# First layer's memory attention: all 512 queries of a head pair in one value run, staged in the base inversion's buffer

## Chip, core and metric

The kernel runs on one core of one Trainium2 chip. Times are device microseconds (us) of one execution. The core has five engines, each with an instruction stream of its own that is worked off in order: TensorE (PE, with its weight loads shown as PEld), VectorE (DVE), ScalarE (ACT), GpSimd (POOL) and SyncE (SP), which here issues most DMAs. An instruction waits on semaphores that other engines or landed DMAs raise; while it waits, all that stands behind it on its engine waits too.

## What is computed

Two layers over 512 positions of width 1024. The first layer mixes the positions with six heads of a gated delta rule (chunks of a triangular system that must be inverted, then a scan over the chunks), the second with sliding-window attention. Each layer also lets every position attend, with four heads of width 64, to 256 memory tokens:

```python
def memory_attention(q, mem_k, mem_v):
    s = jnp.einsum("bshd,bmhd->bhsm", q, mem_k).astype(jnp.float32) * (MEM_DH ** -0.5)
    p = jax.nn.softmax(s, axis=-1).astype(q.dtype)
    o = jnp.einsum("bhsm,bmhd->bshd", p, mem_v)
    return o.reshape(q.shape[0], q.shape[1], MEM_W)
```

Behind the mixers stand an output projection, a gated feed-forward block, and at the end an RMS norm.

## The kernel before

A large product is done in three reduced-precision (fp32r) matmuls of 512 columns each (`mm3`, called from `project` and `normed`): an ACT copy makes the high part of a weight (`whi`), a DVE subtraction the low part (`wlo`), both in `split`. The projections of the first layer are accumulated in three PSUM banks `pj`. Small products (attention, delta rule) are plain fp32 matmuls, which the profile lists as two entries each; transposes are listed as one. They go to the banks `g` (two) and `sc` (three). All instructions are issued in the order of the Python calls and then rearranged by the framework's scheduler into one fixed order per engine; `nosync` adds order without a wait.

The stage around the change is in `gdn`:

- `base_inverse` (lines 690 to 727) inverts the 32x32 diagonal blocks of all 24 chunk systems at once. Its tile `big` (96 of 128 partitions used, 2048 floats wide) holds the blocks in its first half and the inverse X in its second. 31 steps of two DVE operations each (`btmp<-big`, `big<-big,btmp`) run one behind the other, mixed with other DVE work; then ACT copies X transposed into the first half (`big<-big`), and two DMAs on SP, `basex` and `basext` (line 713), store both halves to memory, from where the solve fetches them (`X64`, `Tt`, lines 720 and 725).
- `scores` makes the memory scores of a pair of heads: eight matmuls `mk,qm` into two `g` and two `sc` banks, row maxima on DVE (line 819), exponentials on ACT (L134).
- `weigh` calls `softmax` (the reciprocal) and `weighed`. In `weighed`, for each of four blocks of 128 queries: `scale` divides the weights (two tiles on DVE, line 868, or on ACT), four PE transposes (L150) turn them into a `g` bank, and one ACT copy evicts the bank into `pf`. Before the change, every two blocks four value matmuls `sc<-pf,mv` of 256 columns follow. `split` then makes the pair's result `mq` (high part on ACT, low part on DVE); it is read much later, by the output projection.
- `memory(m, ...)` runs this for the pair m = 0 and m = 1; `query` (lines 608 to 621) makes the intra-chunk products of a head (`g<-qv,kn`, then `DT<-g,DT` on DVE), `conv_tile` the convolution (one ACT copy, three DVE taps, L156), followed by a Silu on ACT.
- `solve` follows (32x32 and 64x64 products `sc<-X,N`, `sc<-Tt,Y`, with DVE evictions between them), then `values` and the scan.

The second layer (`own` true, since its banks are named `pt`) already takes all four blocks in one run of 512 columns, from a tile `pfm`.

## Time and profile before

| quantity | value |
|---|---|
| time, median of 3 runs | 1159.31 us (1158.9 to 1159.67) |
| span of the profiled execution, first to last instruction | 1155.8 us |
| what the median has over that span | 3.5 us |
| PE busy | 1142.6 us (99%) |
| DVE, ACT, POOL busy | 834.0, 626.7, 86.0 us |

The profiled execution's own total is not listed beside its span; the three timed runs lie 3.1 to 3.9 us above the span. In the rows of the timeline, the first number is the start in us from the span's start, the second the length, then engine, source line, operation, out<-in by the program's names, shapes and count; in brackets the idle time of the engine before it and who ended it. A PE entry is long because it includes the pipeline; what a matmul costs is the distance to the next entry's start.

### The profile page before, as it was taken

The numbers are of one execution on the slowest core, as the hardware profiler recorded it, in microseconds if no ns is written. First come the engines' busy times: TensorE is split into PE (matmuls) and PEld (weight loads), VectorE is DVE, ScalarE is ACT, GpSimd is POOL, SyncE is SP. The second block draws the span as 40 slices with busy tenths as digits, with TensorE's granted clock in tenths as the row PEclk, the third lists the DMA queues.
The fourth block names the chain that finished last, engine by engine and source line by source line (L and its number), as shares of the span: only waits on it lengthen the run. The fifth ranks groups of instructions, "written<-read, shape, count | busy, mean of one in ns | idle before, by whom it ended". The sixth has DMA issues, their size and how long they took to land.

```text
span 1155.8 us, 19296 instructions
## 1 busy us (share of the span) xinstructions
PE 1142.6 (99%) x7342; PEld 997.1 (86%) x7342; DVE 834.0 (72%) x1559; ACT 626.7 (54%) x1249; POOL 86.0 (7%) x97
## 2 busy tenths in 40 slices
PE   9999999999999999999999999999999999999996
PEld 7788777877899998899998877788899988999886
DVE  5664886767889877488965777839989644889554
ACT  6489672366566642266653554856666412666433
POOL 0230000000101101011100000001111000111000
PEclk9999999999999999999999999999999999999998
DMA  8244341225657636367623421117577533676232
GB/s 314 84 150 116 131 119 66 95 88 164 188 128 182 169 103 168 114 168 187 154 82 99 124 72 42 51 56 200 131 181 184 151 96 107 170 185 153 78 98 85
DMA packets 72559, 151.20 MB, mean 131 GB/s; under 512 B 16732, under 2 KB 18932, under 8 KB 72468
## 3 DMA queue, kind: packets, MB, share of 16 engines
q1 hardware_dynamic: 61060, 129.28, 35.9%
q0 software_dynamic: 11136, 20.45, 11.2%
q8 instruction: 57, 0.93, 0.3%
q14 instruction: 34, 0.28, 0.1%
q10 hardware_dynamic: 272, 0.26, 0.1%
HBM read 143.00 MB, written 6.96 MB: 130 GB/s over the span
## 4 chain that ended last, share of the span: by engine, by line
PE 93%; DVE 3%; ACT 2%; DMA 1%; issue 0%; SPq 0%; DVEq 0%; ACTq 0%
PE pj L146 43%; PE g L146 38%; PE sc L146 6%; PE qk L146 3%; PE pt L146 2%; PE pt L150 1%; PE g L150 1%; DMA wraw<-in_wmk 1%; ACT sm L134 1%; DVE qv L156 1%; DVE big L153 0%; DVE wlo L153 0%; ACT T L140 0%; DVE btmp L153 0%; DMA wraw<-in_wdn 0%
## 5 line engine op out<-in xcount | busy, mean ns | idle before, releaser
L140 ACT ACTIVATE whi<-wraw 128x512 fp32r<-128x512 f32 (+3 forms) x324 | 240.9, 750 | 254.5 <-PE pj L146 159.2
L153 DVE TENSOR_TENSOR wlo<-wraw,whi 128x512 fp32r<-128x512 f32 (+3 forms) x324 | 270.4, 844 | 100.7 <-ACT whi L140 95.2
L146 PE MATMUL pj<-h,whi 128*128 128x512 f32 (+1 forms) x652 | 257.4, 396 | 0.0
L146 PE MATMUL pj<-l,whi 128*128 128x512 f32 (+1 forms) x652 | 255.0, 392 | 0.0
L146 PE MATMUL pj<-h,wlo 128*128 128x512 f32 (+1 forms) x652 | 254.1, 391 | 0.0
L146 PE MATMUL g<-T,whi 128*128 128x256 f32 x1216 | 220.6, 282 | 0.8 <-ACT fs L140 0.8
L146 PEld LDWEIGHTS g<-T,whi 128*128 128x128 f32 x1216 | 186.9, 189 | 2.1 <-DVE fu L156 1.1
L146 PE MATMUL g<-T,wlo 128*128 128x256 f32 x608 | 171.1, 281 | 0.0
L146 PEld LDWEIGHTS pj<-h,whi 128*128 128x128 f32 x652 | 122.4, 188 | 28.6 <-issue 3.6
L146 PE MATMUL g<-h,whi 128*128 128x256 f32 (+1 forms) x500 | 146.5, 293 | 0.0
L146 PE MATMUL g<-h,wlo 128*128 128x256 f32 (+1 forms) x500 | 145.8, 292 | 0.0
L146 PE MATMUL g<-l,whi 128*128 128x256 f32 (+1 forms) x500 | 145.5, 291 | 0.0
L146 PEld LDWEIGHTS pj<-h,wlo 128*128 128x128 f32 x652 | 122.5, 188 | 25.3 <-issue 0.6
L146 PEld LDWEIGHTS pj<-l,whi 128*128 128x128 f32 x652 | 122.6, 188 | 25.2 <-issue 1.1
L146 PEld LDWEIGHTS g<-T,wlo 128*128 128x128 f32 x608 | 114.4, 188 | 0.0
L146 PEld LDWEIGHTS g<-h,whi 128*128 128x128 f32 x500 | 95.0, 190 | 2.3 <-issue 0.5
L146 PEld LDWEIGHTS g<-l,whi 128*128 128x128 f32 x500 | 94.9, 190 | 2.3 <-issue 0.5
L146 PEld LDWEIGHTS g<-h,wlo 128*128 128x128 f32 x500 | 95.0, 190 | 1.7
L1125 POOL DMA_DIRECT2D ws<-in_wgu x38 | 33.3, 875 | 712.5 <-ACT h L140 447.7
L140 ACT ACTIVATE whi<-ws 128x512 fp32r<-128x512 f32 x76 | 48.0, 631 | 49.1 <-PE g L146 41.4
L153 DVE TENSOR_TENSOR fu<-pj,rstd 128x512 f32<-128x512 f32 (+1 forms) x34 | 22.4, 660 | 53.7 <-PE pj L146 53.7
L153 DVE TENSOR_TENSOR wlo<-ws,whi 128x512 fp32r<-128x512 f32 x76 | 52.2, 687 | 7.4 <-ACT whi L140 7.2
(381 smaller groups left out, 1701.1 us busy)
## 6 DMA issues: line engine op xcount, KB each, us to landing
wraw<-in_wgu SPq DMA_DIRECT2D x50, 512.0 KB, 4.2
ws<-in_wgu SPq DMA_DIRECT2D x76, 256.0 KB, 3.6
ws<-in_wgu POOLq DMA_DIRECT2D x76, 256.0 KB, 4.7
wraw<-in_win SPq DMA_DIRECT2D x26, 512.0 KB, 3.6
wraw<-in_wdn SPq DMA_DIRECT2D x32, 384.0 KB, 3.1
wraw<-in_wdn SPq DMA_DIRECT2D x32, 320.0 KB, 3.0
wraw<-in_wgu SPq DMA_DIRECT2D x38, 256.0 KB, 4.3
wraw<-in_wout SPq DMA_DIRECT2D x16, 512.0 KB, 3.6
```

Of the source, the lines that this page charges most:

```text
L134: ins = self.nc.scalar.activation(out, in_, func, **kw).ins
L140: self.copied = self.nc.scalar.activation(out, in_, AF.Copy, **kw).ins
L146: return self.nc.tensor.matmul(out, lhsT, rhs, start=start, stop=stop, skip_group_check=more).ins
L150: return self.nc.tensor.transpose(out, in_, self.ident[:k, :k]).ins
L153: return eng.tensor_tensor(out=out, in0=a, in1=b, op=op).ins
L156: return self.nc.vector.scalar_tensor_tensor(out=out, in0=in0, scalar=scalar, in1=in1, op0=op0, op1=op1).ins
L1125: nc.gpsimd.dma_start(s1, a22, accum_op=ALU.add)
```

## The change

In the first layer a pair's four blocks are now one group: four value matmuls of 512 columns behind all sixteen transposes, instead of two times four of 256 columns behind eight transposes each. The transposed weights are no longer put into a tile `pf` of 1024 floats a partition (two such in turn for a pair, one buffer), but into a tile of 2048 floats that takes the tag, and so the one buffer, of the base inversion's `big`. The framework adds the waits that this needs: the first eviction into the buffer waits until both stores, `basex` and `basext`, have read it. The second layer's path keeps its tile and group.

```diff
-        group = NC if own else 2
+        group = NC
         for n in range(NC):
             if n % group == 0:
-                pf = {} if win else self.t(pool, [P, 2, 2, group * P], F32, "pfm" if own else "pf", 1)
+                pf = {} if win else self.t(pool, [P, 4 * T], F32, "pfm" if own else "big", 1).rearrange(
+                    "p (j b t) -> p j b t", j=2, b=2)
```

In the instruction order of the built programs, PE has eight matmuls fewer, no engine has any instruction more, and the orders differ between the first pair's transposes and the scan of the first three heads; around those, PE, DVE, ACT and SP are in the same order as before.

## Prediction

> **What bounds the kernel now.** I read the page first: the span, the busy shares, the granted clock and the chain that ended last.

> ```profile
> span 1155.8 us, 19296 instructions
> PE 1142.6 (99%) x7342; PEld 997.1 (86%) x7342; DVE 834.0 (72%) x1559; ACT 626.7 (54%) x1249; POOL 86.0 (7%) x97
> ...
> PEclk9999999999999999999999999999999999999998
> ...
> PE 93%; DVE 3%; ACT 2%; DMA 1%; issue 0%; SPq 0%; DVEq 0%; ACTq 0%
> ```

> PE is the bound: every microsecond that it works less or stands less is gained, every new stop is lost. So two questions count: how much PE work goes, and where PE stops in the new order. Next, the stage by windows (columns: window, length, busy time with entries in brackets of PE, PEld, DVE, ACT, POOL, then clock, DMA share, GB/s).

> ```profile
> 137.00:152.50 15.50, 15.44 (x83) 11.54 (x82) 15.05 (x34) 7.23 (x11) 0.00 (x0) 1.00 0.34 110
> 152.50:165.00 12.50, 11.90 (x67) 9.60 (x66) 10.29 (x27) 11.28 (x26) 0.00 (x0) 1.00 0.68 156
> ```

> The first pair's values run in the first window, while DVE is full (15.05 of 15.50) with the base inversion. The second window holds the inversion's end, the stores and the second pair's scores; there PE shows gaps. The second pair's values follow behind it.

> **Value matmuls.** PE timeline, a run of 256 columns and the entry behind it, and the second layer's run of 512 columns:

> ```profile
> 142.02 1.08 PE L146 MATMUL sc<-pf,mv 128*64 128x256 f32 x8
> 143.04 0.50 PE L146 MATMUL pj<-l,whi 128*128 128x512 f32 x1
> ...
> 712.57 1.94 PE L146 MATMUL pt<-pfm,mv 128*64 128x512 f32 x8
> 714.43 1.79 PE L146 MATMUL qk<-ks,q 64*128 64x128 f32 x16
> ```

> Start to next start, a 256 run costs 1.02, two of them 2.04; the 512 run costs 1.86. That is 0.18 less for a pair, **-0.36** for both. [...] PE goes between fp32r and fp32 matmuls 221 times in both built orders, so I count no change there; three excursions go from this stage and come back in the solve. At 0.2 to 0.3 each this leaves 0.6 either way.

> **The new wait.** The first pair's third and fourth transposes need the `g` banks that hold the first and second; these are evicted into `big`; and that eviction waits for both stores. When does PE arrive, and when does the wait end?

> ```profile
> 137.90 0.48 PE L146 MATMUL pj<-h,whi 128*128 128x512 f32 x1
> ...
> 143.84 0.40 PE L146 MATMUL pj<-l,whi 128*128 128x512 f32 x1
> ...
> 152.24 0.39 PE L146 MATMUL pj<-h,wlo 128*128 128x512 f32 x1
> ```

> The eight transposes are done at 137.90 in both orders. Behind them the new order has 105 projection matmuls (four projections of 24, nine of a fifth). From 143.84 to 152.24 37 of them went: 0.227 each. PE arrives at 137.9 + 23.8, about **161.8**.

> ```profile
> 144.54 0.68 DVE L153 TENSOR_TENSOR mq0l<-sc,mq0h 128x512 fp32r<-128x512 f32 x1
> 145.14 0.36 DVE L153 TENSOR_TENSOR btmp<-big 96x207 f32<-96x207 f32 x1
> ...
> 148.86 1.21 DVE L153 TENSOR_TENSOR wlo<-wraw,whi 128x1024 fp32r<-128x1024 f32 x1
> 149.99 0.29 DVE L153 TENSOR_TENSOR big<-big,btmp 96x135 f32<-96x135 f32 x1
> 150.20 0.74 DVE L156 SCALAR_TENSOR_TENSOR qv<-pj,gains,qv 128x511 f32<-128x511 f32 x1
> 150.86 0.26 DVE L153 TENSOR_TENSOR btmp<-big 96x112 f32<-96x112 f32 x1
> ...
> 155.57 0.18 DVE L153 TENSOR_TENSOR big<-big,btmp 96x31 f32<-96x31 f32 x1
> ```

> The inversion ended at 155.75. A 512-wide DVE operation takes 0.60 of the queue, a weight's low part 1.13, a tap 0.66. Ahead of the inversion's last step the new order loses `mq0l` and one product (-1.20) and gains two taps, one product and one low part (+3.05): 157.6 at most. Some of it falls into the short gaps between dependent steps, so I take 157.5.

> ```profile
> 140.68 1.11 ACT L140 ACTIVATE pf<-g 128x512 f32<-128x512 f32 x2 [1.00 <-PE sc L146]
> ...
> 154.77 0.62 ACT L619 ACTIVATE sq<-qv 128x512 f32<-128x512 f32 x1
> 155.78 1.99 ACT L140 ACTIVATE big<-big 96x1024 f32<-96x1024 f32 x1 [0.39 <-DVE big L153]
> 158.35 0.63 ACT L134 ACTIVATE qv<-qv 128x512 f32<-128x512 f32 x1 [0.58 <-DVE nm L160]
> 159.00 1.28 ACT L125 ACT_TABLE_LOAD   x1
> ...
> 160.76 0.47 ACT L134 ACTIVATE sm<-g,nm 128x256 f32<-128x256 f32 x1
> ```

> The stores, from the list of DMA issues (size, median us from issue to landing), with the fastest and the commonest DMA of this stage beside them:

> ```profile
> wraw<-in_win SPq DMA_DIRECT2D x26, 512.0 KB, 3.6
> ...
> q<-sq SPq DMA_DIRECT2D x6, 256.0 KB, 2.0
> ...
> basext<-big SPq DMA_DIRECT2D x1, 384.0 KB, 3.1
> ```

> On ACT, a Silu (0.63), a table load (1.28) and a square (0.62) now stand ahead of the transposing copy; the last tap that the Silu needs has one 512-wide product and seven small inversion steps (0.2 to 0.3 each) behind it on DVE, so it lies some 2.3 us ahead of the inversion's end, and the three are through at about 157.7. The copy takes 1.99, to 159.7; the `basext` store needs 3.1 more: **162.8**. An eviction takes 0.6 (two in 1.11, the second overlapping), and PE goes on at about 163.4: a stop of 1.65 us. Further on, the third eviction holds up a query product and, in the second pair, the last eviction the value run, 0.2 each: **+2.05**. The unknown is the store: it may land as early as a 256 KB store (2.0) or as late as a median weight load (3.6), which moves the stop from 0.55 to 2.15.

> Cover of the wait elsewhere: ACT waits in front of the eviction with the later evictions, the pair's high part and the second pair's exponentials behind it. No DVE work but the second pair's depends on these. The stores' SP queue has two weight loads ahead of them, for buffers freed before the inversion ends, and the `X64` fetches behind, which the solve needs some 20 us later: nothing.

> **Waits that go, and waits that come back.** PE around the second pair's scores, and the same scores of the first pair, which nothing hindered:

> ```profile
> 124.12 1.14 PE L146 MATMUL g<-mk,qm 64*128 64x256 f32 x8
> ...
> 126.05 0.50 PE L146 MATMUL pj<-h,whi 128*128 128x512 f32 x1
> ...
> 152.47 2.09 PE L146 MATMUL g<-qv,kn 128*128 128x128 f32 x16
> 154.85 0.91 PE L146 MATMUL g<-mk,qm 64*128 64x256 f32 x3 [0.30 <-DVE DT L153]
> ...
> 157.89 0.50 PE L146 MATMUL pj<-h,whi 128*128 128x512 f32 x1
> ...
> 163.47 1.05 PE L146 MATMUL g<-qv,kn 128*128 128x128 f32 x8
> 164.82 0.30 PE L150 MATMUL g<-consts,sm 128*128 128x128 f32 x1 [0.30 <-DVE sm L868]
> ```

> And the query products as a group (busy us, mean ns of one entry):

> ```profile
> L146 PE MATMUL g<-qv,kn 128*128 128x128 f32 x48 | 6.1, 277 | 0.0
> ```

> Unhindered, the scores take 1.93. Here they take 3.04 (154.85 to 157.89), so 1.1 is waiting. The sixteen entries of the query products at 152.47 start 0.12 apart (2.09 less the last one's 0.28, over 15), so the next could have started at 154.4, not 154.85: 0.45 lost, of which the row shows 0.30 as idle. By the same count 0.45 is lost ahead of 164.82. Together **-2.0** of stops in the old order that the new one does not have in these places. But it has its own: the second `g` bank of the scores waits for the second product on DVE, now behind one more 512-wide operation (0.60, plus the ACT copy that it needs), about 0.7 in all; and the third query product stands right behind the scores instead of behind 24 projection matmuls, so PE waits for one maximum (0.60), a small scaling (0.1) and two exponentials (0.47 each), less five scores (0.24 each): about 0.5 to 0.6. **+1.3**.

> **Behind the solve** the new order differs too:

> ```profile
> 208.61 0.91 PE L146 MATMUL pj<-h,wlo 128*128 128x512 f32 x2
> 209.36 0.39 PE L146 MATMUL pj<-h,whi 128*128 128x512 f32 x1
> ```

> DVE beside it, the evictions of the last solve step:

> ```profile
> 205.92 1.26 DVE L160 TENSOR_SCALAR Tt<-sc 64x256 f32<-64x256 f32 x3
> ```

> Before, nine projection matmuls stood beside DVE's three evictions (1.26), one tap (0.66) and a low part (1.13), 3.05 in all, and 0.3 was lost (0.75 for two entries of 0.227). In the new order seven projection matmuls and four transposes follow the solve's twelve matmuls, about as much PE work, while DVE has the three evictions, three taps (2.0) and the low part: 4.4, which is 1.3 more. I take 1.2 lost instead of 0.3, **+0.9**, between 0.4 (the taps fall into DVE's own waits) and 1.4 (none does).

> **Sum:** -0.36 + 2.05 - 2.0 + 1.3 + 0.9 = **+1.9 us** on the span of 1155.8, so 1157.7. The median of the runs lies 3.5 above this span (1159.31), so I predict **1161.2**.

> **Rivals.**
> *Waits do not bind* (faster): the stores land before PE arrives, the score chain's old stops (2.0) go and no new ones come, the solve stays covered. Then -0.36 - 2.0 gives 1156.9. For the store to land by 161.2 and be evicted by 161.8, ACT's copy must begin by 156.1, so the inversion must end 1.4 us earlier than I work out, and the Silu, the table load and the square must not stand ahead of it. DVE's fill, 15.05 of 15.50, speaks against it; that the old order had the inversion's end at 155.75 speaks for it. If the store alone comes in time and the rest is as computed, the sum is +0.25: 1159.6.
> *The wait is long*: the stores meet the loads of a window whose DMA share is 0.68 already and land 1.5 to 2 later, or each of the three re-placed chains costs half as much again: +3.5 to +5, about 1163.5.
> *PE slows down after the stop*: if a stop made the clock fall, matmuls of 0.227 would take longer; at half speed the fourteen projection matmuls that stand behind the scores cost 3.2 more, 1164.4. The clock's row shows nothing like it and the stage's windows have 1.00. [...]

> **How the numbers follow.** The computed case has 0.62; the store in time with the rest as computed 0.16; the long wait 0.14; the slower clock 0.02; no binding waits 0.06. The forecast's terms move it by about 1.5 either way (store 1.1 down and 0.5 up, excursions 0.6, the solve's 0.5). With the case below it and half of the long wait, the range is 1159.0 to 1163.6. A difference of 0.2% (2.3 us) is about what a measurement of this kernel can tell from no change: slower means above 1161.6, which is a third of the computed case, the long wait and the clock, 0.38; faster means below 1157.0, 0.04; within it 0.58.

> **What would show it.** In the changed profile: value runs of 512 columns at about 1.86; the inversion's last step at about 157.5; ACT's eviction into `big` ended by the `basext` DMA at about 162.8, and PE idle ahead of an L150 transpose, released by ACT, for 1 to 2 us; a gap ahead of the query product behind the second scores; a gap behind the solve at about 205 to 211. It is wrong if the stores land before 161 or PE's gap exceeds 2.5, and if PE's windows from 137 to 215 together move by less than 0.8 or more than 3.2.

## The result and the profile after

| quantity | before | after |
|---|---|---|
| time, median of 14 executions each | 1158.89 us (1157.97 to 1160.07) | 1161.99 us (1160.77 to 1169.93) |
| ratio, 95% interval | | 1.0045 (1.0035 to 1.0054) |
| span of the profiled execution | 1155.8 us | 1159.6 us |

The change costs time, clear of noise. The medians are 3.1 us apart, which is 0.27%; the ratio takes in all executions and lies nearer to that of the means (1163.85 and 1158.93). The forecast was 1161.2, with "within 0.2%" as the likeliest sign: the median lies in the range, but it is slower than that sign allowed. Two things stand beside the median. Every execution of the new kernel takes its span plus 1.7 to 1.9 us (1161.4 for the profiled one), while the prediction carried over 3.5 us from before. In the later executions of the kernel before, whose spans are on record, it is 1.7 to 2.9; so part of the 3.5 was that the profiled execution of before was a short one. And the executions of the new kernel scatter over 9 us, those of before over 2.

The page of the kernel after: PE is busy about as long as before (1143.4 us for 1142.6), but the span is 3.8 longer.

```profile
span 1159.6 us, 19269 instructions
PE 1143.4 (99%) x7326; PEld 996.4 (86%) x7326; DVE 835.1 (72%) x1559; ACT 626.4 (54%) x1249; POOL 85.1 (7%) x97
```

The same two windows as in the prediction (columns: window, length, busy time with entries of PE, PEld, DVE, ACT, POOL, then clock, DMA share, GB/s):

```profile
137.00:152.50 15.50, 15.50 (x74) 12.98 (x73) 15.18 (x32) 7.18 (x10) 0.00 (x0) 1.00 0.38 117
152.50:165.00 12.50, 10.33 (x51) 8.31 (x49) 9.26 (x20) 8.97 (x11) 0.00 (x0) 1.00 0.65 176
```

The first window has no gap left, the second lost 1.6 us of PE work (11.90 before). The timeline of PE shows where:

```profile
161.47 0.39 PE L146 MATMUL pj<-h,wlo 128*128 128x512 f32 x1
164.03 1.15 PE L150 MATMUL g<-consts,sm 128*128 128x128 f32 x8 [2.17 <-ACT big L140]
...
166.24 1.94 PE L146 MATMUL sc<-big,mv 128*64 128x512 f32 x8
168.10 1.38 PE L146 MATMUL g<-qv,kn 128*128 128x128 f32 x10
169.42 1.13 PE L146 MATMUL g<-mk,qm 64*128 64x256 f32 x4
...
172.65 1.16 PE L146 MATMUL g<-qv,kn 128*128 128x128 f32 x8
```

The stop sits where it was expected, ahead of the third transposes and released by ACT's eviction into `big`; start to start it is 2.56, which less one matmul (0.227) leaves 2.33. The run of 512 columns costs 1.86 (168.10 less 166.24). The second pair's scores take 3.23 (172.65 less 169.42), against 3.04 before and 1.93 where nothing hinders them. What DVE and ACT did before the stop:

```profile
157.07 0.19 DVE L153 TENSOR_TENSOR big<-big,btmp 96x31 f32<-96x31 f32 x1
```

```profile
157.56 2.11 ACT L140 ACTIVATE big<-big 96x1024 f32<-96x1024 f32 x1
...
162.03 0.67 ACT L140 ACTIVATE qv<-pj,gains 128x512 f32<-128x512 f32 x1
163.38 1.09 ACT L140 ACTIVATE big<-g 128x512 f32<-128x512 f32 x2 [0.67 <-ACT qv L140]
```

```profile
basext<-big SPq DMA_DIRECT2D x1, 384.0 KB, 3.6
```

The inversion ended at 157.3, the copy at 159.7; the store, issued then, took 3.6 and landed at about 163.3; the eviction began at 163.38. (The row names ACT's own operation as the releaser, but that had been done for 0.67 us: the store is what came last.)

Behind the solve, PE and DVE:

```profile
210.35 0.40 PE L146 MATMUL pj<-l,whi 128*128 128x512 f32 x1
211.03 0.47 PE L146 MATMUL pj<-h,whi 128*128 128x512 f32 x1 [0.28 <-ACT qv L140]
...
211.66 0.66 PE L150 MATMUL g<-consts,qv 128*128 128x128 f32 x4
212.98 0.50 PE L146 MATMUL pj<-h,wlo 128*128 128x512 f32 x1 [0.66 <-DVE wlo L153]
```

```profile
208.49 0.42 DVE L160 TENSOR_SCALAR Tt<-sc 64x256 f32<-64x256 f32 x1 [0.61 <-PE sc L146]
...
211.71 1.21 DVE L153 TENSOR_TENSOR wlo<-wraw,whi 128x1024 fp32r<-128x1024 f32 x1
```

From DVE's first eviction (208.49) to the end of the low part's slot (212.84, where the next operation starts) are 4.35 us; PE loses 0.45 and 0.92 there.

What the stage costs in all is read from an operation that both kernels have ahead of it and one behind it, on DVE: before first, then after.

```profile
125.09 1.23 DVE L153 TENSOR_TENSOR wlo<-wraw,whi 128x1024 fp32r<-128x1024 f32 x1 [0.41 <-ACT whi L140]
...
241.09 1.23 DVE L153 TENSOR_TENSOR wlo<-wraw,whi 128x1024 fp32r<-128x1024 f32 x1 [0.81 <-ACT whi L140]
```

```profile
124.98 1.22 DVE L153 TENSOR_TENSOR wlo<-wraw,whi 128x1024 fp32r<-128x1024 f32 x1 [0.67 <-ACT whi L140]
...
244.19 1.23 DVE L153 TENSOR_TENSOR wlo<-wraw,whi 128x1024 fp32r<-128x1024 f32 x1 [1.27 <-ACT whi L140]
```

It is later by 3.10 behind the stage and earlier by 0.11 ahead of it: **+3.2 us** in the stage, where the prediction had +1.9. The span's remaining 0.6 arises in the second layer. ACT there waits for a weight load; before, then after:

```profile
785.26 1.06 ACT L140 ACTIVATE whi<-wraw 128x1024 fp32r<-128x1024 f32 x1 [2.02 <-DMA wraw<-in_wout]
```

```profile
789.13 1.06 ACT L140 ACTIVATE whi<-wraw 128x1024 fp32r<-128x1024 f32 x1 [2.77 <-DMA wraw<-in_wout]
```

The load came 0.76 later against its surroundings (3.87 between these rows, 3.10 between the DVE rows above). This is not scatter of single executions: the distance from the second DVE row to this one is 544.9 to 545.8 us in fourteen traces of kernels told of here that merge both pairs (the changed one ten times, the copy apart twice, the third store, the merge in its own tile), and 544.15 to 544.24 in the five traces of kernels that leave the first pair as it was (before, its control, the second pair alone, the buffer without the merge twice). So this part comes with the merge of the first pair, also where no store is waited for. Its cause is open: behind the stage PE, DVE, ACT and POOL have the same order of instructions in both kernels.

### The profile page after: what moved, and what is told of

It is laid out like the page before. It is cut to its first block, busy times and chain, and to the rows that moved or that the text cites. A ratio compares the mean times of both kernels' runs of the same rounds, so it can differ in the third digit from the quotient of the medians.

```text
span 1159.6 us, 19269 instructions
## 1 busy us (share of the span) xinstructions
PE 1143.4 (99%) x7326; PEld 996.4 (86%) x7326; DVE 835.1 (72%) x1559; ACT 626.4 (54%) x1249; POOL 85.1 (7%) x97
## 4 chain that ended last, share of the span: by engine, by line
PE 92%; DVE 3%; ACT 2%; DMA 2%; issue 1%; SPq 0%; DVEq 0%; ACTq 0%
PE pj L146 42%; PE g L146 38%; PE sc L146 6%; PE qk L146 3%; PE pt L146 1%; PE pt L150 1%; DVE wlo L153 1%; PE g L150 1%; DMA wraw<-in_wgu 1%; DMA wraw<-in_wmk 1%; DVE qv L156 1%; ACT whi L140 0%; ACT sm L134 0%; DMA wraw<-in_wout 0%; DVE btmp L153 0%
## 5 line engine op out<-in xcount | busy, mean ns | idle before, releaser
L140 ACT ACTIVATE whi<-wraw 128x512 fp32r<-128x512 f32 (+3 forms) x324 | 240.9, 750 | 253.0 <-PE pj L146 161.6
L153 DVE TENSOR_TENSOR wlo<-wraw,whi 128x512 fp32r<-128x512 f32 (+3 forms) x324 | 271.2, 846 | 102.0 <-ACT whi L140 94.4
L146 PE MATMUL pj<-h,whi 128*128 128x512 f32 (+1 forms) x652 | 257.5, 397 | 0.3 <-ACT qv L140 0.3
L146 PE MATMUL pj<-l,whi 128*128 128x512 f32 (+1 forms) x652 | 254.9, 391 | 0.3 <-DVE l L156 0.3
L146 PE MATMUL pj<-h,wlo 128*128 128x512 f32 (+1 forms) x652 | 254.3, 391 | 0.7 <-DVE wlo L153 0.7
L146 PE MATMUL g<-T,whi 128*128 128x256 f32 x1216 | 220.6, 282 | 0.9 <-ACT fs L140 0.9
L146 PEld LDWEIGHTS g<-T,whi 128*128 128x128 f32 x1216 | 186.9, 189 | 2.2 <-DVE fu L156 1.1
L146 PE MATMUL g<-T,wlo 128*128 128x256 f32 x608 | 171.1, 281 | 0.0
L146 PEld LDWEIGHTS pj<-h,whi 128*128 128x128 f32 x652 | 122.4, 188 | 29.3 <-issue 4.0
L146 PE MATMUL g<-h,whi 128*128 128x256 f32 (+1 forms) x500 | 146.6, 293 | 0.0
L146 PE MATMUL g<-h,wlo 128*128 128x256 f32 (+1 forms) x500 | 145.8, 292 | 0.0
L146 PE MATMUL g<-l,whi 128*128 128x256 f32 (+1 forms) x500 | 145.5, 291 | 0.0
L146 PEld LDWEIGHTS pj<-h,wlo 128*128 128x128 f32 x652 | 122.5, 188 | 25.4 <-DVE wlo L153 0.9
L146 PEld LDWEIGHTS pj<-l,whi 128*128 128x128 f32 x652 | 122.6, 188 | 25.2 <-issue 0.7
L146 PEld LDWEIGHTS g<-T,wlo 128*128 128x128 f32 x608 | 114.5, 188 | 0.0
L146 PEld LDWEIGHTS g<-h,whi 128*128 128x128 f32 x500 | 95.0, 190 | 2.3 <-issue 0.5
L146 PEld LDWEIGHTS g<-l,whi 128*128 128x128 f32 x500 | 94.9, 190 | 2.3 <-issue 0.5
L146 PEld LDWEIGHTS g<-h,wlo 128*128 128x128 f32 x500 | 95.0, 190 | 1.8
L140 ACT ACTIVATE whi<-ws 128x512 fp32r<-128x512 f32 x76 | 48.0, 631 | 48.8 <-PE g L146 41.0
L153 DVE TENSOR_TENSOR fu<-pj,rstd 128x512 f32<-128x512 f32 (+1 forms) x34 | 22.4, 660 | 54.6 <-PE pj L146 54.6
L153 DVE TENSOR_TENSOR wlo<-ws,whi 128x512 fp32r<-128x512 f32 x76 | 52.1, 686 | 7.3 <-ACT whi L140 7.2
## 6 DMA issues: line engine op xcount, KB each, us to landing
wraw<-in_wgu SPq DMA_DIRECT2D x50, 512.0 KB, 4.2
ws<-in_wgu SPq DMA_DIRECT2D x76, 256.0 KB, 3.5
ws<-in_wgu POOLq DMA_DIRECT2D x76, 256.0 KB, 4.8
wraw<-in_win SPq DMA_DIRECT2D x26, 512.0 KB, 3.6
wraw<-in_wdn SPq DMA_DIRECT2D x32, 384.0 KB, 3.0
wraw<-in_wgu SPq DMA_DIRECT2D x38, 256.0 KB, 4.4
wraw<-in_wout SPq DMA_DIRECT2D x16, 512.0 KB, 3.5
```

The lines of the kernel that those rows point to most:

```text
L140: self.copied = self.nc.scalar.activation(out, in_, AF.Copy, **kw).ins
L146: return self.nc.tensor.matmul(out, lhsT, rhs, start=start, stop=stop, skip_group_check=more).ins
L153: return eng.tensor_tensor(out=out, in0=a, in1=b, op=op).ins
```

## The experiments

The theory ahead of them, T: the loss is PE's stops, above all the wait of the evictions for the stores. Rival M: the merged run itself costs time, since four evictions must be done before it. Rival C: a stop lets PE's clock fall, and this makes the scatter. "In the stage" below means the same difference of DVE operations, from 125 to about 241.

### The second pair alone

```diff
# against the changed kernel
-        group = NC
+        group = NC if own or m else 2
-                pf = ... self.t(pool, [P, 4 * T], F32, "pfm" if own else "big", 1)
+                pf = ... self.t(pool, [P, 4 * group * P], F32, "pfm" if own else "big" if m else "pf", 1)
```

> The change for the second pair alone: the first pair keeps its two groups of two blocks and its own tile. PE's order differs from before only in where the second pair's value run stands. The second pair's evictions come long after both stores. Wait theory: no new stop, 0.18 saved: 1158.7, between 1158.4 and 1159.0. Rival (a merged run costs by itself, since all four evictions must be done before it): 0.3 to 0.8 slower than before, 1159.2 to 1159.7.

Measured: 1156.91 (11 executions, 1156.48 to 1157.51) beside 1158.04 of before; ratio 0.9989 (0.9980 to 0.9997). It is the only version that beats both kernels. The second pair's evictions go into `big` too, but long after the stores, and PE does not stop for them:

```profile
168.69 0.40 PE L146 MATMUL pj<-h,wlo 128*128 128x512 f32 x1
169.06 1.94 PE L146 MATMUL sc<-big,mv 128*64 128x512 f32 x8
170.93 0.50 PE L146 MATMUL pj<-h,whi 128*128 128x512 f32 x1
```

The run costs 1.87 and stands between projections; the stage is 0.25 shorter than before, close to the 0.18 a pair. The rest of the 1.1 us by which the median is lower has no row: the executions of before that it is compared with scatter over 2 us, and one trace of each was taken. Sharing the buffer cost nothing here, where the stores are old (1.87 for the run, no idle time ahead of it). For the second pair M falls.

### Both pairs merged, without the wait

A four-block tile of its own takes 4 KB a partition more than `pf`, so three buffers were made smaller to make room, in a control and in the merged kernel alike.

```diff
# control: the kernel before with
-"btmp", 2   "qv", 5   "R", 3
+"btmp", 1   "qv", 4   "R", 2
# merged: the changed kernel with the same, and
-"pfm" if own else "big", 1
+"pfm" if own else "pf", 1
```

> Control: the kernel before the change with three buffers made smaller (btmp one instead of two, qv four instead of five, R two instead of three), which frees 3.5 KB a partition. PE's order differs in a dozen rows. By every theory 1158 to 1159, within 0.05% of the kernel before, and no execution with a mean clock below 0.996.

> The changed kernel's four-block groups for both pairs, but with a tile of their own of 2048 floats (tag pf) instead of the inversion's buffer, made possible by the control's smaller buffers: the merge without the wait. PE's order is that of the control but for the place of the value runs. Wait theory: the control less 0.36 us, so 1157.6 to 1158.6, and no execution with a low clock. Rival (it is the merging and the new order of evictions that cost): as the changed kernel, 1161 or more.

Measured: control 1158.22 (1157.13 to 1159.80), ratio 1.0004 (0.9995 to 1.0013); merged 1158.29 (1157.73 to 1159.06), ratio 1.0003 (0.9994 to 1.0012). The merge without the shared buffer costs nothing and gains nothing that shows: in the traces the stage is 0.25 shorter than the control's, less than the 0.36 expected, and the load in the second layer comes 0.77 later (544.97 for 544.20 of the distance above), so that little is left in the time. No execution of either has a mean clock below 0.997. In the stage M falls for the first pair too, and the loss of 3 us hangs on the first pair's use of `big`, that is, on the wait and on the order that the scheduler makes around it.

### The buffer without the merge

```diff
# the kernel before, with
-pf = ... self.t(pool, [P, 2, 2, group * P], F32, "pfm" if own else "pf", 1)
+pf = ... self.t(pool, [P, 4 * T], F32, "pfm" if own else "big", 1)[:, :4 * group * P] (rearranged)
```

> Only the buffer of the change: two groups of two blocks as in the kernel before, 256-column runs, but their tile is the base inversion's big. Wait theory: the stop behind the store is there as in the changed kernel (about 2.3), and the value runs are 0.36 dearer: 1161.5 to 1162.2. Rival (the merged run itself delays the pair's result and costs the time): 1158.9 to 1159.3, as before the change.

Measured: 1164.78 (1163.46 to 1168.50), ratio 1.0067 (1.0054 to 1.0080): T's direction, 3 us more than it gave. The trace says why. The stop is that of the changed kernel, and behind it the clock is at half:

```profile
162.08 0.39 PE L146 MATMUL pj<-h,wlo 128*128 128x512 f32 x1
164.54 0.70 PE L150 MATMUL g<-consts,sm 128*128 128x128 f32 x4 [2.07 <-ACT big L140]
165.18 1.98 PE L146 MATMUL sc<-big,mv 128*64 128x256 f32 x8
...
169.53 1.08 PE L146 MATMUL sc<-big,mv 128*64 128x256 f32 x8
```

```profile
164.00:165.00 1.00, 0.46 (x4) 1.00 1.09 171
165.00:166.00 1.00, 1.00 (x6) 0.51 0.89 140
...
169.00:170.00 1.00, 1.00 (x8) 1.00 0.91 369
```

(The columns: window, length, PE busy with entries, granted clock, DMA share, GB/s.) The same eight entries of 256 columns take 1.98 at a clock of 0.50 and 1.08 at 1.00. C is seen for the first time: the fall behind the stop. All six executions have mean clocks of 0.990 to 0.996. Another execution of this kernel (1163.04) had the fall in the same place:

> The kernel before with only its buffer changed (two groups of two, in big), one look; two of its six executions were above 1168. Theory A and B as for repeat_e: a long fall at 185 to 230 for A, from 164 on for B; an execution of 1163.5 to 1164.2 would show the fall of 3.4 us behind the stop, as the first look did.

### A shorter wait

```diff
# against the changed kernel
-        Xt = big(0)
+        Xt = self.t(gp, [P, 2 * T], F32, "xt", 1)[:n, :e] (rearranged)
```

> The changed kernel with the inversion's transposed copy in a tile of its own, so that the first eviction into big waits for the first store only (issued at about 157.3, 3.1 us) and for ACT's copy. Wait theory: the store lands at about 160.4; PE arrives at about 159.9 (eight projection matmuls of 0.227 fewer stand ahead of the transposes), goes on at about 161.1, a stop of 1.1 instead of 2.3, and the time is about 1160.2, 1.2 below the changed kernel. Clock theory: besides this no execution above 1162, since the stop is too short. Rival (the loss comes from the new order behind the stop, not from the store): 1161.4 as before, the stop only moved.

Measured: 1161.67 (1160.83 to 1167.20), ratio 1.0041 (1.0025 to 1.0058). The stop shrank only to 1.65 idle, because ACT had a product and a high part ahead of the eviction, and it began at 161.47 though the first store had long been issued (157.7):

```profile
157.95 2.10 ACT L140 ACTIVATE xt<-big 96x1024 f32<-96x1024 f32 x1
159.95 0.67 ACT L140 ACTIVATE qv<-pj,gains 128x512 f32<-128x512 f32 x1
160.52 1.04 ACT L140 ACTIVATE whi<-wraw 128x1024 fp32r<-128x1024 f32 x1
161.47 1.06 ACT L140 ACTIVATE big<-g 128x512 f32<-128x512 f32 x2
```

No idle time stands ahead of the last row: ACT's order is what releases PE here, not the store. In the stage the kernel is 1.0 faster than the changed one; in the time nothing of it is seen, and two of six executions were at 1166 and 1167, where none above 1162 was expected. But the stop isn't shown to be what slowed them: in the two traces of this kernel, a slow execution among them (below), the clock stays up behind the stop.

### A longer wait

```diff
# against the changed kernel: one store more (third_store);
# round_trips has two fetches into big and two stores more in its place
+        d = self.t(self.dpool, [NH, NB, BASE * BASE], F32, "again")
+        nc.sync.dma_start(d..., Xt...)
```

> The changed kernel with one more store of the transposed copy (384 KB, to a scratch that nobody reads) behind the two, so that the first eviction into big waits for three stores. Wait theory: the stop ahead of the transposes grows from 2.2 to between 3.3 and 5, and the time by as much, to 1162.5 to 1164.5 where the clock stays up. Clock theory: with a stop this long nearly every execution has PE's clock at half for 3 us or more behind the stop, as the windows of the kernel with halves in big show from 165 to 168; a fall of 3.2 us at half speed costs 1.6 us more, so that the median is 1165 or above and the trace shows windows of 0.50 right behind the stop. If the clock stays at 1.00 in the trace and the executions agree within 1 us, the stop's length isn't what lets the clock fall.

Measured: 1161.85 (1161.25 to 1167.82), ratio 1.0042 (1.0026 to 1.0058); the trace has 1.85 idle ahead of the transposes and a clock of 1.00. The stop did not grow: the new order put more projections ahead of it. The experiment tells nothing of a longer stop.

> The changed kernel with two more fetches of the stored copy back into big and two more stores of it behind the two (what they write is read by nobody), a chain of four more transfers of some 3 us, so that the first eviction into big comes some 12 us later. The program's order puts some 43 more projection matmuls (9.8 us) ahead of the waiting transposes, so the stop should be 4 to 6 us instead of 2.2. Clock theory (a stop lets the clock fall by chance of its length and its place in time): with 4 us or more every execution has the clock at 0.50 behind the stop, the mean clock is 0.996 or less in all six, and the executions stand within 1 us or fall into steps. Rival (the stop has nothing to do with it): as often as in the changed kernel, one in three.

Measured: 1173.01 (1171.61 to 1176.72; mean clocks 0.985 to 0.987). The stop ahead of the first transposes was again 2.07 long, but this order has one of 3.43 further on and long gaps in the solve. The windows are cut at the clock's edges:

```profile
188.50:191.38 2.88, 0.14 (x2) 1.00 0.01 3
191.38:198.20 6.82, 5.55 (x24) 0.50 0.10 38
...
205.00:208.44 3.44, 2.77 (x88) 1.00 0.02 5
208.44:225.50 17.06, 16.34 (x218) 0.50 0.04 11
```

The first fall comes after 2.9 us in which PE did next to nothing, the second after 3.4 us in which it was busy for 2.77 with 88 entries. The clock stays at half for 6.8 and for 17.1 us, that is two and five times 3.41, and the second fall covers the second half of the solve and what stands behind them.

### The changed kernel again, to find where the clock falls

The changed kernel unedited, and further executions of two kernels told of above.

> The changed kernel once more, nothing edited. Wait theory (the loss is PE's stops: 2.3 us ahead of the first pair's third transposes, about 1.3 around the second pair's scores, about 1.6 behind the solve, against about 2.5 of stops of the old order, and 0.36 saved): about 1161.4 us in most executions, the DVE operations behind 240 us some 3.1 later than before, and the same idle of about 2.2 ahead of a transpose at 164. Clock theory (the stop sometimes lets PE's granted clock fall, and that is what makes some executions 1165 to 1170): executions above 1163 with a mean clock of 0.994 or less come again, and a trace of one shows windows below 1.00 from about 164 on. If the later executions have the clock fall at another place (the first 30 us or the end), the clock theory is wrong.

> The changed kernel once more, one look, for a trace of an execution with a low clock: about one execution in three had a mean clock of 0.994 or less. Clock theory: if this is one, the windows from 164 on are at 0.50 for as long as the missing time says (time above 1161.4, doubled: 6 us more would be 12 us at half speed, in one piece or several). If it isn't one, it tells only how the stop ahead of the transposes (2.2 to 2.3 so far) and the load that was late at 785 in the second layer repeat.

> The changed kernel, one look. Clock theory: a stop of 2.1 to 2.4 ahead of the transposes; either no window below 1.00 and a time of 1161 to 1162, or 0.50 for about 3.3 us behind the stop and 1163 (as in repeat_b), or, in an execution of 1165 to 1170, 0.50 for 8 to 17 us.

> As repeat_c, for another execution: of the three kinds (clock up, 0.50 for 3.3 us, 0.50 for 8 to 17 us) the last hasn't been seen in a trace; two chances of about one in three.

> The changed kernel, one look, to meet an execution of 1165 to 1170 (about three in ten). Theory A (the long falls start behind the solve, where the kernel with round trips shows 0.50 from 208.7 to 222: small matmuls with gaps don't bring the clock back): in such an execution the clock is 1.00 or 0.50 for 3.3 us behind the first stop, and 0.50 for 8 us or more somewhere from 185 to 230. Theory B (they start at the stop at 162 and last): 0.50 in one piece from 164 on for 8 us or more.

> As repeat_e, for another execution; if the time is 1161 to 1163, the traces should again be of the two kinds already seen: 1.00 throughout, or 0.50 for about 3.4 us behind the stop at 162 to 164.

> The changed kernel with the transposed copy in its own tile, one look, to meet one of its executions of 1165 to 1167 (two of six). Its stop ahead of the transposes is shorter (1.8) while the gap behind the solve is as in the changed kernel. Theory A: a long fall at 185 to 230 and none, or one of 3.4 us, behind the stop at 160 to 162. Theory B: in one piece from 162 on.

> The changed kernel, one look, to meet one of its own executions of 1165 to 1170. The look at the kernel with the transposed copy apart showed a long fall that began at 201.9, inside the solve, with PE busy all through, and lasted 17.0 us, five times the short fall's 3.4. Theory A: in the changed kernel too the long fall starts inside or behind the solve (190 to 215), lasts a multiple of 3.4 us, and costs some 6 us. Theory B: it starts at 164.

> As repeat_g, for another execution. If it is of 1161 to 1163: no fall, or one of 3.4 us from 164 to 165 on that costs 1.3 to 1.6 us.

> As repeat_g and repeat_h, for a third execution: no fall at 1161 to 1162, a fall of 3.4 us behind the stop at 1162.5 to 1163.5, a long one inside or behind the solve at 1165 to 1170.

The first of these gave 1162.6 (1161.38 to 1166.96), ratio 1.0041 (1.0029 to 1.0054); its trace had no fall, as that of the changed kernel itself. The single executions: 1163.12, 1162.59, 1161.88, 1162.08, 1161.72, 1166.38, 1162.52 and 1162.43 (b to i), and 1167.33 for the copy apart. The traces are of three kinds. No fall: d, e, f. A fall of 3.4 us right behind the stop: b, c, h, i, which makes the stage 1.25 to 1.6 longer than in the first trace after the change. In b:

```profile
161.15:164.56 3.41, 1.31 (x7) 1.00 0.99 228
164.56:167.98 3.42, 3.42 (x17) 0.50 1.06 163
```

A long fall inside the solve: g, where the part behind is 5.2 later than in the trace without a fall:

```profile
200.13:203.54 3.41, 3.41 (x94) 1.00 0.00 0
203.54:217.18 13.64, 13.64 (x65) 0.50 0.00 1
```

and the kernel with the copy apart, where the part behind is 6.2 later than in its first trace:

```profile
198.41:201.82 3.41, 3.41 (x92) 1.00 0.00 0
201.82:218.88 17.06, 16.92 (x100) 0.50 0.00 1
```

Neither had a fall at its stop, 40 us earlier. Theory A of the expectations holds and B doesn't: both executions above 1165 whose traces were met have their fall in the solve. All 28 executions of the changed kernel put together: 12 from 1160.8 to 1162.1 with mean clocks of 0.997 or 0.998, 9 from 1162.4 to 1163.4 with 0.996, 7 from 1165.0 to 1169.9 with 0.989 to 0.994. Of 62 executions of the kernel before none is above 1160.07, and none has a mean clock below 0.997 where it is on record.

Why does the same stop let the clock fall in four traces of ten and not in the others? In these traces the clock changes only at places that lie whole multiples of 3.41 us apart. In b it comes back at 167.98 and falls for the last time, behind the last work, at 1154.43: 986.45 us, which is 289 times 3.4133. This last fall is in every trace, so each trace shows where its windows of 3.41 us begin, also one without another fall. In the first trace after the change:

```profile
1152.38:1155.79 3.41, 0.00 (x0) 1.00 0.53 172
1155.79:1159.20 3.41, 0.00 (x0) 0.50 0.41 136
```

Counted back from there, the windows lie differently against the stop in each execution. The window that holds most of the stop, in c (a fall behind it), in e (none), and in the first trace of the copy apart (none; its whole stop of 1.65 us lies in this window):

```profile
161.99:165.40 3.41, 1.45 (x10) 1.00 0.95 188
160.83:164.24 3.41, 1.60 (x8) 1.00 0.91 230
158.84:162.25 3.41, 1.76 (x9) 1.00 0.72 196
```

This sorts the ten traces of the changed kernel. In the four with a fall behind the stop, PE is busy for 1.31 (b), 1.33 (i), 1.35 (h) and 1.45 us (c) of that window. In the six others the stop is divided between two windows, and the emptier one has 1.60 (e), 1.77 (g), 1.89 (the first trace), 1.95 (f), 2.06 (d) and 2.15 (the first repeat). The two traces of the buffer without the merge have 1.34 and 1.32, and both fall. In all twenty traces every window at full clock with less than 1.6 us of PE's work is followed by a fall, and outside the solve none with 1.76 or more is; at 1.6 it went both ways (none in e, the last fall in b behind 1.61). So in these traces the clock falls behind the stop or not by where the stop lies among the windows. An estimate from these figures: some 1.8 us of it (3.41 less 1.6) have to lie in one.

## Why the prediction was wrong

The mechanism was seen, but the loss was sized too small: +1.9 us on the span was forecast, and +3.8 was measured in a trace in which the clock did not fall. The steps that failed are the store's term, and with it the stop; the solve and the second layer, which had no term; and the rival of the clock, which was all but ruled out.

- **Value runs**: right. 1.86 for 512 columns in both pairs, -0.36; and the second pair alone shortened the stage by 0.25.
- **The new wait, up to the store**: right. PE arrived at 161.7 (161.8), the inversion ended at 157.3 (157.5), the copy at 159.7 (159.7).
- **The store**: mis-sized. The 3.1 was taken from before; here it took 3.6. The stop became 2.33 instead of 1.65, just beyond the upper end of 2.15 that the prediction gave.
- **Stops of the old order that go, new ones around the scores**: right in the sum, -2.0 and +1.3 (3.23 less 1.93). They were placed a little differently: most of the 1.3 stands within the scores, little ahead of the query product behind them.
- **Behind the solve**: right in its working (4.35 on DVE against 4.4), 1.4 lost, less 0.3 of before: +1.1 for 0.9.
- **The excursions between kinds of matmul**: the rows above give -0.36 + 2.33 + 0.2 - 2.0 + 1.3 + 1.1 = +2.6, with 0.2 for the small waits behind the stop; +3.2 was measured. About as much as the other 0.6 is found in the solve, where no row of the prediction stands. Its first matmuls and its last run, before and then after:

```profile
181.83 1.20 PE L146 MATMUL sc<-X,N 32*32 32x32 f32 x48
...
205.12 1.61 PE L146 MATMUL sc<-Tt,Y 64*64 64x64 f32 x24
```

```profile
185.43 1.20 PE L146 MATMUL sc<-X,N 32*32 32x32 f32 x48
...
207.78 1.61 PE L146 MATMUL sc<-Tt,Y 64*64 64x64 f32 x24
```

Between these starts the old order takes 23.29 us with 41 projection matmuls, the new one 22.35 with 34; less 0.227 for each, 13.98 and 14.63, which is 0.65 more. PE leaves the projections 14 times there instead of 12. In the whole stage it is 40 times in both orders, as the prediction said; that an excursion costs more in the solve than where it went is likely and not shown. (For one the prediction took 0.2 to 0.3; before shows 0.2 at the first pair's scores: 0.32 from the last projection matmul ahead, at 123.80, to the first score, and 0.34 from the first one behind, at 126.05, to the next, together 0.2 over two of 0.227.)
- **The second layer**: the prediction counts no change there. It was 0.6 on the span.
- **The offset from span to median**: 3.5 was carried over; the new median lies 2.4 above the span of the profiled execution. This hid 1.1 of the 1.9 by which the span was missed (1159.6 for 1157.7). That the median lies 0.8 from the forecast is luck. (The chance of "slower" has a small slip: a third of 0.62 with 0.14 and 0.02 is 0.37, not 0.38.)
- **"PE slows down after the stop", 0.02**: this step failed too. The half speed that it reckons with is what the traces show: the clock is at 0.50 in the trace of before too, from 1149.81 on, behind the last work. It was put aside because the clock stood at 1.00 in the stage and the stop was taken to be 1.65 long; that a stop of this length leaves the clock up was the author's estimate, and no run had shown it. In the traces taken later each has its windows of 3.41 us at a place of its own, and 1.31 to 1.45 us of work in the window with the stop did not keep the clock up (b, i, h, c). The two errors hang together: the stop of 1.65 in the kernel with the copy apart left the clock up although it lay in one window (1.76 us of work), while the stop behind the longer store (3.6 for 3.1) let it fall in four traces of ten. In place of one fall at a price of 3.2, 16 of 28 executions have a mean clock of 0.996 or less. A fall behind the stop cost 1.25 to 1.6, one in the solve, which the prediction doesn't have, 5 to 6. Of the result's own fourteen executions the seven with a mean clock of 0.997 or more have a median of 1161.4, so the falls add 0.6 to the median.

Why the solve lets the clock fall only in the new order is open. PE is busy all through there, with 32x32 and 64x64 tiles. Between the solve's first and last matmul the kernels that never took longer than 1160.1 (before, its control, the second pair alone, the merge in its own tile) have 41 projection matmuls; the changed kernel and the copy apart have 34, the buffer without the merge 35, the third store 29. The place of the window counts here too: in g three projection matmuls begin in the window ahead of the fall; in the first trace the window lies 0.13 us later in the same order, a fourth begins in it, and the clock stays up. But in the control a window with two of them among small matmuls (192.17 to 195.58) was not followed by a fall, so their number alone doesn't decide. A solve with more full-size work at the same order was not tried.

## What to carry to other kernels

Before a tile takes over a buffer, look at who reads it last: if that is a DMA store, its landing, at the length that stores have in that window, ends the first write's wait (here 3.6 us behind the copy), and the same merge with the buffer free cost nothing that shows in the time (1158.29 beside 1158.22). Where PE is the bound, price a new stop by more than its length: here a stop of 2.1 us of idle time cost another 1.25 to 1.6 by the clock in some executions, one of 1.65 cost nothing more, and a fall among small matmuls cost 5 to 6. Ask how much of a stop can lie in one of the windows that the traces show, here of 3.41 us. Look at the scatter and the mean clocks of many executions, not at one trace, and take the offset from span to time from the span and the time of the same execution.
